# Waits of GpSimd behind VectorE, and sums that read PSUM, in a two-layer attention trunk on one core

## The chip, the core and the metric

The kernel runs on one core of a Trainium2 chip. A core has engines with queues of their own that run side by side: TensorE (PE in the rows; PEld is its weight load), VectorE (DVE), ScalarE (ACT), GpSimd (POOL) and SyncE (SP), which issues the DMA transfers here. SBUF is the working memory of all of them, PSUM the memory into which TensorE writes; this kernel uses it as eight banks of 128 x 512 fp32. The metric is the device time of one execution in microseconds (us); three executions of the kernel before took 1012.47, 1005.16 and 1011.17 us, median 1011.17.

## The reference

The input is x, 256 x 1024 in fp32. There are two layers, and each adds three things to x: a SwiGLU feed-forward of 1024 to 2816 to 1024, a mixer, and a second feed-forward, every one between two RMS norms. Layer 1's mixer is plain attention over 16 heads with a bias by distance. Layer 0's mixer, the even one, is where the change lies. One projection h @ w_in (1024 to 3368 columns) gives:

- A: four differential heads. Each has two query and two key vectors of 64 and one value of 128. With p1 and p2 the two masked softmaxes, the weights are p1 - lam * p2.
- B: eight heads of 64 that look at the best 64 keys alone, as an indexer chooses them (8 small heads of 32, relu, a weighted sum, top 64).
- Queries and keys of A, B and the indexer are turned by rotary embedding first.

```
def apply_rope(x, cos, sin):
    x1, x2 = jnp.split(xf, 2, axis=-1)
    return jnp.concatenate([x1 * c - x2 * s, x2 * c + x1 * s], axis=-1)

s = jnp.einsum('bqhcd,bkhcd->bhcqk', qblk, kf) * scale
p = masked_softmax(s, mask)
w = p[:, :, 0] - lam * p[:, :, 1]
```

## The kernel before, in words

Every matrix product is made of three fp32r products: a high and a low part of each operand, high x high, high x low and low x high. So each weight tile passes ScalarE, which casts it to a high part wh (L277), and then VectorE, which makes the low part wl = raw - wh (L279). In the even mixer wl may be made by VectorE or by GpSimd, 512 columns at a time. The 256 tokens are two tiles t of 128.

Nothing is written down in the order in which it runs. The program calls op(engines, us, fn, w, r, pos, port) for each piece of work, which records it with an estimated duration and a due place pos. Plan.issue then plays the whole list through on estimated durations: an engine that is free takes, of the pieces that are ready and whose buffers are free, the one due first, and its instruction is issued. An instruction thus stands in its engine's queue where that play put it, and on the chip each queue runs in that fixed order and waits at semaphores for its inputs. The buffers are counted: `ps` has 4 PSUM banks and `y` 4.

One rule of the planner concerns the change. VectorE and GpSimd are taken to share a port to SBUF. A piece marked port=True is not begun in the play while another marked piece runs on either engine:

```
if o["port"] and e != "ACT" and port > now + 1e-9:
    fits = False
    event(port, "", None)
```

This orders the estimated times alone. On the chip no wait stands between the two engines for it.

Marked pieces are the wl subtractions (L279), products and sums of two SBUF tensors in the norms (L471, L529, L544, L550, L555), the scaling of softmax weights in B (L841), the sum at the end of rope (L744) and the sum of a differential head (L983).

rope (L729 on) takes a projection's PSUM bank b. L736 writes b * cos to an SBUF tile a, two L740 write the sine parts to an SBUF tile r, and L744 adds r to a; the planner chooses VectorE or GpSimd for the sum. TensorE transposes the sum (L427) into another bank, and ScalarE and VectorE split that into high and low parts (L363/L365, L369/L371). Ten ropes are computed: two of 288 columns for the indexer (after which GpSimd copies 96 columns, L894) and eight of 512.

A differential head h takes its scores (L795) in two banks of `ps`. soft() adds the mask and takes the negated maximum (L812, VectorE, from PSUM to an SBUF tile e), then the exponentials with their sums (L816, ScalarE, in place in e). The pieces L977 to L979 work on columns of 128 x 2 in SBUF and carry no mark; L983 adds the second softmax times a factor to the first, in SBUF. Then come the transposes of the sum (L427), their split (L369, pt) and the product with the values (L417 to L419, y<-blk,pt).

Within the even mixer VectorE also makes the indexer's scores (L923) and takes the top 64 in eight rounds of L930 and L931 for each t; these have one SBUF tensor as input, or PSUM and SBUF.

Of the kernel before, what the change touches and what calls it, by code (L numbers as in the profile page):

```python
# [14 lines left out]
P = 128  # L15
# [37 lines left out]
class Plan:  # L53
# [36 lines left out]
        self.pos += us  # L90
        return self.last

    def issue(self):
        free = dict(SLOTS)
        eng = {e: 0.6 for e in LAT}
        heap = {e: [] for e in LAT}
        ev, n, port = [], 0, 0.0
        todo = len(self.ops)

        def push(o):  # L100
            for e in o["eng"]:
                heapq.heappush(heap[e], (o["pos"], o["id"], o))

        def event(t, kind, x):
            nonlocal n
            n += 1
            heapq.heappush(ev, (t, n, kind, x))

        for o in self.ops:
            if o["n"] == 0:  # L110
                push(o)
        event(0.6, "", None)
        now = 0.0
        while ev:
            now = ev[0][0]
            while ev and ev[0][0] <= now + 1e-9:
                _, _, kind, x = heapq.heappop(ev)
                if kind == "ready":
                    push(x)
                elif kind == "free":  # L120
                    free[x.tag] += x.n
            for e in heap:
                if eng[e] > now + 1e-9:
                    continue
                skip, got, late = [], None, None
                while heap[e]:
                    z = heapq.heappop(heap[e])
                    o = z[2]
                    if o["end"] is not None:
                        continue  # L130
                    need = [q for q in o["refs"] if q.t is None]
                    fits = all(free[q.tag] >= sum(p.n for p in need if p.tag == q.tag) for q in need)
# [4 lines that stand above are left out]
                    for q in o["refs"]:  # L137

                        if q.tag in BANKS and q.used[0] != e and q.used[1] > now + 1e-9:
                            fits = False  # L140
                            event(q.used[1], "", None)
                    if fits and o["safe"] <= now + 1e-9:
                        got = o
                        break
                    if fits and late is None:
                        late = z
                    skip.append(z)
                if got is None and late is not None:
                    got = late[2]
                    skip.remove(late)  # L150
                for z in skip:
                    heapq.heappush(heap[e], z)
                if got is None:
                    continue
                o = got
                need = [q for q in o["refs"] if q.t is None]
                for q in need:
                    free[q.tag] -= q.n
                    q.t = q.make()
                us = o["us"] if len(o["eng"]) == 1 else o["us"][e]  # L160
                o["fn"]() if len(o["eng"]) == 1 else o["fn"](e)
                if o["port"] and e != "ACT":
                    port = now + us
                end = eng[e] = o["end"] = now + us
                todo -= 1
                event(end, "", None)
                for q in o["refs"]:
                    q.used = (e, end + 0.1)
                for d in o["out"]:
                    d["n"] -= 1  # L170
                    at = end + (OWN[e] if d["eng"] == (e,) else o["lat"])
                    d["ready"] = max(d["ready"], at)
                    if d["eng"] == ("PE",) != (e,):
                        d["safe"] = max(d["safe"], at + SAFE)
                    if d["n"] == 0:
                        d["ready"] = max(d["ready"], now)
                        event(d["ready"], "ready", d)
                for q in o["refs"]:
                    q.left -= 1
                    if q.left == 0:  # L180
                        event(end + 0.05, "free", q)
        assert todo == 0, [(o["eng"], o["pos"], o["n"], [q.tag for q in o["refs"]])
                           for o in self.ops if o["end"] is None][:20]
        return now
# [6 lines left out]
def n_dve(n, fast=False):  # L191
    return 0.07 + n * (0.00052 if fast else 0.00104)
# [3 lines left out]
def trunk_kernel(  # L196
# [531 lines left out]

    def rope(b, tab, t, n, half, fa, fk):  # L729

        g = n // (2 * half)
        a, r = t2(), t2()
        v4 = lambda q: q.t[:, :n].rearrange("p (g two h) -> p g two h", two=2, h=half)
        def c1():
            c = tab.t[:, t, 0, :].rearrange("p (two h) -> p two h", two=2).unsqueeze(1).to_broadcast([P, g, 2, half])
            nc.vector.scalar_tensor_tensor(v4(a), v4(b), fa(), c, op0=ALU.mult, op1=ALU.mult)  # L736
        op(DVE, n_dve(n) + 0.06, c1, r=[b, tab] + fk, w=[a])
        def c2(i):
            s = tab.t[:, t, 1, i * half:(i + 1) * half].unsqueeze(1).to_broadcast([P, g, half])
            nc.vector.scalar_tensor_tensor(v4(r)[:, :, i, :], v4(b)[:, :, 1 - i, :], fa(), s, op0=ALU.mult, op1=ALU.mult)  # L740
        for i in range(2):
            op(DVE, n_dve(n // 2) + 0.06, lambda i=i: c2(i), r=[b, tab] + fk, w=[(r, i)])
        def add(e):
            (nc.vector if e == "DVE" else nc.gpsimd).tensor_add(a.t[:, :n], a.t[:, :n], r.t[:, :n])  # L744
        op(DVE + POOL, {"DVE": n_dve(n), "POOL": 0.11 + n * 0.00233}, add, r=[(r, 0), (r, 1)], w=[a], port=True)
        return a

    class HL:

# [53 lines left out]

        op(ACT, 1.4, lambda: nc.scalar.activation(warm.t, nhalf.t[:, 0:1], fn), r=[nhalf], w=[warm], after=after)

    def soft(bs, hh, madd, mk, r, c, pos):

        e = t2()
        mx = sm(2)
        for t in range(2):  # L810
            def mxf(t=t):
                nc.vector.tensor_tensor_reduce(e.t[:, QS[t]], bs[hh].t[:, QS[t]], madd(t), -1.0, 1e38, ALU.add, ALU.min,  # L812
                                               mx.t[:, t:t + 1])
            op(DVE, n_dve(KL[t]), mxf, r=[(bs[hh], t)] + mk, w=[(e, t), (mx, t)], pos=pos)
            def ex(t=t):
                nc.scalar.activation(e.t[:, QS[t]], e.t[:, QS[t]], AF.Exp, bias=mx.t[:, t:t + 1], scale=-1.0,  # L816
                                     accum_out=r.t[:, c + t:c + t + 1])
# [61 lines left out]
    def even(xT, nxt):  # L879
# [90 lines left out]
        for h in range(4):  # L970
            pos = pA + h * PERA
            r, ri = sm(4), sm(4)
            bs = scores(aq.v, aq.k(0) + aq.k(1), h, h, pos, trs[h - 2:h - 1] if h > 1 else ())
            es = [soft(bs, c, cm, [cmask], r, 2 * c, pos) for c in range(2)]
            def comb(h=h, ri=ri, r=r):

                nc.vector.reciprocal(ri.t[:, 2:4], r.t[:, 2:4])  # L977
# [3 lines left out]
            for t in range(2):  # L981
                def ad(t=t, e=es, ri=ri):
                    nc.vector.scalar_tensor_tensor(e[0].t[:, QS[t]], e[1].t[:, QS[t]], ri.t[:, 2 + t:3 + t],  # L983
                                                   e[0].t[:, QS[t]], op0=ALU.mult, op1=ALU.add)
                op(DVE, n_dve(KL[t]) + 0.06, ad, r=[ri, (es[1], t)], w=[(es[0], t)], pos=pos, port=True)
            z = new_pt(1)
            trs.append(transp_p(es[0], z, 0, pos))
            def pv(h=h, z=z):
# [131 lines left out]
    for l in range(2):  # L1120
        for p in range(3):
# [11 lines left out]
            else:  # L1133
                ffn(l, p // 2, xT, nxt)
            xT = z
    pl.issue()


# [48 lines left out]
```

## Time and profile before

| what | before |
|---|---|
| three executions | 1012.47, 1005.16, 1011.17 us; median 1011.17 us |
| the profiled execution | 1006.86 us |
| its span, first to last instruction | 1005.1 us |
| TensorE busy | 991.6 us, 99% of the span |
| VectorE, ScalarE, GpSimd busy | 725.7, 607.4 and 85.2 us |
| DMA moved | 185.52 MB, 185 GB/s |
| mean granted clock of TensorE | 0.999 |

All times of rows are those of the profiled execution, counted from the span's start. A matmul row's length runs past the start of the next matmul, since matmuls are pipelined: where 512-column matmuls follow each other they start 0.23 us apart while each row has 0.39 us. A row with "xN" merges N instructions of the same kind that follow each other. What stands in brackets is how long the engine was idle before the row, and what ended that. The even mixer runs from about 195 to 322 us of the span.

### The profile page before, as it was taken

How to read it: one execution, taken by the hardware profiler on the slowest of the kernel's cores; microseconds unless marked ns; L12 is line 12 of the kernel's file. 1: busy time of each engine (PE TensorE's matmuls, PEld its weight loads, DVE VectorE, ACT ScalarE, POOL GpSimd, SP SyncE). 2: the span in 40 equal slices, each digit the busy share in tenths (PEclk: the TensorE clock that was granted, in tenths of full speed). 3: DMA queues.
4: the chain of work that ended last, by engine and by line, in shares of the span. 5: the costliest groups of instructions: out<-in, count | busy, mean ns of one | idle time of the engine just before them, and what ended most of it. 6: DMA issues, size and time to landing. Idle time of an engine off the chain costs nothing.

```text
span 1005.1 us, 15484 instructions
## 1 busy us (share of the span) xinstructions
PE 991.6 (99%) x5435; PEld 847.6 (84%) x5435; DVE 725.7 (72%) x1537; ACT 607.4 (60%) x1376; POOL 85.2 (8%) x107
## 2 busy tenths in 40 slices
PE   9999999999999999999999999999999999999997
PEld 8888888877888988888888888888888888888886
DVE  7766668689888676677577667676778877666682
ACT  8555556556588555565466555576578856555661
POOL 1000000156531100000020000001100010000000
PEclk9999999999999999999999999999999999999999
DMA  9866665555545567666467666664775447666621
GB/s 343 293 184 178 196 191 144 161 178 167 167 138 157 166 218 200 192 187 190 146 209 247 180 182 192 195 178 149 224 267 159 124 148 251 188 179 194 192 87 42
DMA packets 125933, 185.52 MB, mean 185 GB/s; under 512 B 6040, under 2 KB 93984, under 8 KB 125856
## 3 DMA queue, kind: packets, MB, share of 16 engines
q1 hardware_dynamic: 125856, 184.54, 59.9%
q8 instruction: 42, 0.69, 0.3%
q14 instruction: 35, 0.29, 0.1%
HBM read 183.47 MB, written 1.05 MB: 184 GB/s over the span
## 4 chain that ended last, share of the span: by engine, by line
PE 89%; DVE 7%; ACT 2%; issue 1%; DMA 1%; POOLq 0%; DVEq 0%; ACTq 0%; POOL 0%
PE ps L387 26%; PE ps L389 14%; PE y L417 9%; PE y L418 9%; PE y L419 9%; PE ps L412 4%; PE ps L409 4%; PE ps L410 4%; PE ps L427 2%; DVE wl L279 2%; PE ps L417 2%; PE ps L418 2%; PE ps L419 2%; PE ps L795 1%; DMA g<-in_norm_g_dram 1%
## 5 line engine op out<-in xcount | busy, mean ns | idle before, releaser
L279 DVE TENSOR_TENSOR wl<-raw,wh 128x512 fp32r<-128x512 f32 (+2 forms) x636 | 418.0, 689 | 133.5 <-ACT wh L277 91.3
L277 ACT CAST wh<-raw 128x512 fp32r<-128x512 f32 (+2 forms) x668 | 378.8, 615 | 124.5 <-issue 70.1
L387 PE MATMUL ps<-xT,wh 128*128 128x512 f32 x1152 | 290.4, 393 | 0.0
L387 PEld LDWEIGHTS ps<-xT,wh 128*128 128x128 f32 x1152 | 208.1, 189 | 38.0
L389 PEld LDWEIGHTS ps<-xT,wl 128*128 128x128 f32 x1152 | 157.5, 190 | 11.6
L389 PE MATMUL ps<-xT,wl 128*128 128x256 f32 x1152 | 162.8, 283 | 0.0
L417 PE MATMUL y<-wh,blk 128*128 128x512 f32 x352 | 138.1, 392 | 0.0
L418 PE MATMUL y<-wl,blk 128*128 128x512 f32 x352 | 137.4, 390 | 0.0
L419 PE MATMUL y<-wh,blk 128*128 128x512 f32 x352 | 137.1, 390 | 0.0
L409 PE MATMUL ps<-wh,xT 128*128 128x512 f32 (+2 forms) x320 | 107.6, 351 | 0.1
L410 PE MATMUL ps<-wl,xT 128*128 128x512 f32 (+2 forms) x320 | 106.1, 347 | 0.8 <-DVE wl L279 0.3
L396 DVE TENSOR_TENSOR t<-ps,t 128x256 f32<-128x256 f32 x144 | 60.6, 421 | 44.3 <-ACT t L395 42.8
L395 ACT COPY t<-ps 128x256 f32<-128x256 f32 x144 | 53.6, 373 | 51.8 <-PE ps L389 48.0
L453 POOL TENSOR_TENSOR sm<-sm 128x1 f32<-128x1 f32 x24 | 14.9, 621 | 777.9 <-ACT t L534 721.4
L419 PEld LDWEIGHTS y<-wh,blk 128*128 128x128 f32 x352 | 66.1, 188 | 13.9
L417 PEld LDWEIGHTS y<-wh,blk 128*128 128x128 f32 x352 | 66.2, 188 | 12.8
L418 PEld LDWEIGHTS y<-wl,blk 128*128 128x128 f32 x352 | 66.2, 188 | 12.6
L410 PEld LDWEIGHTS ps<-wl,xT 128*128 128x128 f32 x320 | 60.6, 189 | 8.8 <-DVE wl L279 2.3
L412 PE MATMUL ps<-wh,xT 128*128 128x512 f32 (+2 forms) x320 | 67.6, 347 | 0.0
L409 PEld LDWEIGHTS ps<-wh,xT 128*128 128x128 f32 x320 | 60.5, 189 | 8.0 <-ACT xT L363 0.5
L680 ACT ACTIVATE t<-t 128x256 f32<-128x256 f32 x64 | 26.8, 418 | 55.2 <-DVE t L679 55.2
L412 PEld LDWEIGHTS ps<-wh,xT 128*128 128x128 f32 x320 | 51.3, 189 | 6.6
(148 smaller groups left out, 1030.7 us busy)
## 6 DMA issues: line engine op xcount, KB each, us to landing
raw<-in_wd_dram SPq DMA_DIRECT2D x88, 512.0 KB, 4.2
raw<-in_wg_dram SPq DMA_DIRECT2D x86, 512.0 KB, 4.4
raw<-in_wu_dram SPq DMA_DIRECT2D x86, 512.0 KB, 4.5
raw<-in_ew_in_dram SPq DMA_DIRECT2D x24, 512.0 KB, 4.6
raw<-in_ow_in_dram SPq DMA_DIRECT2D x24, 512.0 KB, 4.5
g<-in_norm_g_dram SPq DMA_DIRECT2D x11, 512.0 KB, 5.7
raw<-in_ew_out_dram SPq DMA_DIRECT2D x8, 512.0 KB, 3.7
raw<-in_ow_out_dram SPq DMA_DIRECT2D x8, 512.0 KB, 4.0
```

The lines of the kernel that those rows point to most:

```text
L277: nc.scalar.copy(ref.t[0][:, sl], raw.t[:, sl])
L279: (nc.vector if e == "DVE" else nc.gpsimd).tensor_sub(ref.t[1][:, sl], raw.t[:, sl], ref.t[0][:, sl].bitcast(F32))
L387: nc.tensor.matmul(b.t, w()[0], xT.both[:, k].rearrange("p j c -> p (j c)"), start=k == 0, stop=False)
L389: nc.tensor.matmul(b.t[:, 0:S], w()[1], xT.t[0][:, k, :], start=False, stop=k == KT - 1)
L395: op(ACT, n_act(S, True), lambda: nc.scalar.copy(dst.t[:, sl], b.t[:, S:512]), r=[b], w=[(dst, sl.start)])
L396: op(DVE, n_dve(S), lambda: nc.vector.tensor_add(dst.t[:, sl], b.t[:, 0:S], dst.t[:, sl]), r=[b], w=[(dst, sl.start)])
L409: nc.tensor.matmul(o(), ah, bh, start=k == 0, stop=False)
L410: nc.tensor.matmul(o(), ah, bl, start=False, stop=False)
L412: nc.tensor.matmul(o(), al, bh, start=False, stop=k == KT - 1)
L417: nc.tensor.matmul(o, ah, bh, start=start, stop=False)
L418: nc.tensor.matmul(o, ah, bl, start=False, stop=False)
L419: nc.tensor.matmul(o, al, bh, start=False, stop=stop)
```

## The change

It has four parts.

1. The planner remembers the last marked instruction that it issued on VectorE (held). Whenever it issues a marked instruction on GpSimd, it adds a dependence on that one, so that GpSimd waits at a semaphore until it has ended. Nothing is added to VectorE's instructions.
2. rope keeps its cosine part in the projection's own bank: the two sine parts are made first, then b is multiplied by cos in place, and the sum r = b + r reads PSUM and SBUF. It is for VectorE alone and has no mark. One SBUF tile less is used; the bank is released after the sum.
3. The second softmax of a differential head stays in its scores' bank: L812 and L816 write where they read. The bank is released after L983.
4. L983 thus reads PSUM and SBUF and loses its mark.

```
-    def issue(self):
+    def issue(self, tc):
...
-        ev, n, port = [], 0, 0.0
+        ev, n, port, held = [], 0, 0.0, None
...
                 if o["port"] and e != "ACT":
                     port = now + us
+                    done = tc.nc.cur_bb.bb.instructions[-1]
+                    if e == "DVE":
+                        held = done
+                    elif held is not None:
+                        tc.add_manual_dep(done, held.name, mybir.DependencyInfo(mybir.DependencyClass.Sync, mybir.DependencyReason.DATA),
+                                          reason="port")
...
     def rope(b, tab, t, n, half, fa, fk):
-        a, r = t2(), t2()
+        r = t2()
...
-            nc.vector.scalar_tensor_tensor(v4(a), v4(b), fa(), c, op0=ALU.mult, op1=ALU.mult)
-        op(DVE, n_dve(n) + 0.06, c1, r=[b, tab] + fk, w=[a])
...
         for i in range(2):
             op(DVE, n_dve(n // 2) + 0.06, lambda i=i: c2(i), r=[b, tab] + fk, w=[(r, i)])
-        def add(e):
-            (nc.vector if e == "DVE" else nc.gpsimd).tensor_add(a.t[:, :n], a.t[:, :n], r.t[:, :n])
-        op(DVE + POOL, {"DVE": n_dve(n), "POOL": 0.11 + n * 0.00233}, add, r=[(r, 0), (r, 1)], w=[a], port=True)
-        return a
...
+            nc.vector.scalar_tensor_tensor(v4(b), v4(b), fa(), c, op0=ALU.mult, op1=ALU.mult)
+        op(DVE, n_dve(n) + 0.06, c1, r=[tab] + fk, w=[b])
+        op(DVE, n_dve(n), lambda: nc.vector.tensor_add(r.t[:, :n], b.t[:, :n], r.t[:, :n]), r=[b], w=[(r, 0), (r, 1), r])
+        return r
...
-    def soft(bs, hh, madd, mk, r, c, pos):
-        e = t2()
+    def soft(bs, hh, madd, mk, r, c, pos, inplace=False):
+        e = bs[hh] if inplace else t2()
...
-            es = [soft(bs, c, cm, [cmask], r, 2 * c, pos) for c in range(2)]
+            es = [soft(bs, c, cm, [cmask], r, 2 * c, pos, c == 1) for c in range(2)]
...
-                op(DVE, n_dve(KL[t]) + 0.06, ad, r=[ri, (es[1], t)], w=[(es[0], t)], pos=pos, port=True)
+                op(DVE, n_dve(KL[t]) + 0.06, ad, r=[ri, (es[1], t)], w=[(es[0], t)], pos=pos)
```

Because the planner's inputs differ, the order differs on four engines, from the start of the even mixer's ropes to its end; SyncE's order is the same. In the changed program lines above the insertion at L164 are shifted: L277 is L284, L279 is L286, L369 and L371 are L376 and L378, L427 is L434; rope's sine parts are L744, its cosine L749, its sum L751; L977 to L979 are L983 to L985, and L983 is L989.

The first place is VectorE's queue between the rope of the indexer's second tile (ps_2186) and that of the first head group's second tile (ps_2235, in the changed program ps_2234). wl, raw and wh are the parts of the weight tiles, blk the split queries. Before:

```order
L740 SCALAR_TENSOR_TENSOR t_371_2245<-ps_2186,sm_2118,r_82 128x9x16 x2
L279 TENSOR_TENSOR wl_2232<-raw_2057,wh_2231 128x512
L279 TENSOR_TENSOR wl_2225<-raw_2036,wh_2224 128x512
L279 TENSOR_TENSOR wl_2232<-raw_2057,wh_2231 128x512
L279 TENSOR_TENSOR wl_2252<-raw_2084,wh_2251 128x512
L279 TENSOR_TENSOR wl_2263<-raw_2129,wh_2262 128x512
L371 SCALAR_TENSOR_TENSOR blk_2268<-ps_2254,blk_2267 128x4x128
L736 SCALAR_TENSOR_TENSOR t_386_2306<-ps_2235,sm_2118,r_81 128x512
L740 SCALAR_TENSOR_TENSOR t_388_2314<-ps_2235,sm_2118,r_81 128x8x32 x2
L744 TENSOR_TENSOR t_386_2306<-t_386_2306,t_388_2314 128x512
```

The changed program there:

```order
L751 TENSOR_TENSOR t_368_2239<-ps_2186,t_368_2239 128x288
L286 TENSOR_TENSOR wl_2222<-raw_2036,wh_2221 128x512
L286 TENSOR_TENSOR wl_2230<-raw_2057,wh_2229 128x512
L286 TENSOR_TENSOR wl_2250<-raw_2084,wh_2249 128x512
L286 TENSOR_TENSOR wl_2261<-raw_2129,wh_2260 128x512
L378 SCALAR_TENSOR_TENSOR blk_2266<-ps_2252,blk_2265 128x4x128
L376 TENSOR_TENSOR blk_2208<-ps_2282,blk_2207 128x3x128
L286 TENSOR_TENSOR wl_2261<-raw_2129,wh_2260 128x512
L744 SCALAR_TENSOR_TENSOR t_385_2317<-ps_2234,sm_2118,r_81 128x8x32 x2
L749 SCALAR_TENSOR_TENSOR ps_2234<-ps_2234,sm_2118,r_81 128x512
L751 TENSOR_TENSOR t_385_2317<-ps_2234,t_385_2317 128x512
```

The indexer's sum, which GpSimd made before, now stands on VectorE ahead of the subtractions, the split of the indexer's second tile has come forward into this stretch, and one of the five subtractions has moved behind it.

The second place is GpSimd's queue over the same stretch. Before:

```order
L744 TENSOR_TENSOR t_354_2157<-t_354_2157,t_356_2173 128x288
L894 COPY t_354_2157<-t_354_2157 128x96
L744 TENSOR_TENSOR t_360_2196<-t_360_2196,t_361_2202 128x512
L279 TENSOR_TENSOR wl_2225<-raw_2036,wh_2224 128x512
L279 TENSOR_TENSOR wl_2252<-raw_2084,wh_2251 128x512
L279 TENSOR_TENSOR wl_2263<-raw_2129,wh_2262 128x512
L744 TENSOR_TENSOR t_370_2240<-t_370_2240,t_371_2245 128x288
L894 COPY t_370_2240<-t_370_2240 128x96
```

The changed program:

```order
L900 COPY t_354_2157<-t_354_2157 128x96
L286 TENSOR_TENSOR wl_2222<-raw_2036,wh_2221 128x512
L286 TENSOR_TENSOR wl_2230<-raw_2057,wh_2229 128x512
L900 COPY t_368_2239<-t_368_2239 128x96
L286 TENSOR_TENSOR wl_2250<-raw_2084,wh_2249 128x512
L286 TENSOR_TENSOR wl_2294<-raw_2169,wh_2293 128x512
```

The sums are gone. By the semaphores of the changed program, wl_2222 there waits for L536 (blk_2189, the product ahead of the second rope), wl_2250 for VectorE's first wl_2261, and wl_2294 for its second.

The third place is VectorE's queue at the sums of differential heads 1 and 2. Before, they stand behind the last round of the second top 64 and its mask (L933), next to each other:

```order
L740 SCALAR_TENSOR_TENSOR t_474_2811<-ps_2693,sm_1963,r_81 128x8x32 x2
L933 TENSOR_SCALAR selm<-t_405_2415 128x256
L983 SCALAR_TENSOR_TENSOR t_441_2640<-t_444_2648,sm_2677,t_441_2640 128x128
L983 SCALAR_TENSOR_TENSOR t_441_2640<-t_444_2648,sm_2677,t_441_2640 128x256
L983 SCALAR_TENSOR_TENSOR t_462_2737<-t_466_2753,sm_2779,t_462_2737 128x128
L983 SCALAR_TENSOR_TENSOR t_462_2737<-t_466_2753,sm_2779,t_462_2737 128x256
L744 TENSOR_TENSOR t_473_2798<-t_473_2798,t_474_2811 128x512
```

In the changed program head 1's sum follows its factors:

```order
L983 RECIPROCAL sm_2688<-sm_2644 128x2
L984 SCALAR_TENSOR_TENSOR sm_2688<-sm_2688,nlam,sm_2644 128x2
L985 TENSOR_TENSOR rsq<-sm_2644 128x2
L378 SCALAR_TENSOR_TENSOR blk_2587<-ps_2582,sm_2118,blk_2586 128x512
L989 SCALAR_TENSOR_TENSOR t_435_2636<-ps_2616,sm_2688,t_435_2636 128x128
L989 SCALAR_TENSOR_TENSOR t_435_2636<-ps_2616,sm_2688,t_435_2636 128x256
L936 MAX m_1_91<-t_400_2413 128x8
```

Head 1's sum has moved ahead of most rounds of the second top 64 (L936 and L937 there), and reads the bank ps_2616.

## Rows read from the trace of the kernel before

**Rows 1.** The page's first part: busy time, share of the span and number of instructions of each engine.

```profile
PE 991.6 (99%) x5435; PEld 847.6 (84%) x5435; DVE 725.7 (72%) x1537; ACT 607.4 (60%) x1376; POOL 85.2 (8%) x107
```

**Rows 2.** The waits of TensorE in the whole span: what waited, for whom, us in total, times, the longest.

```profile
PE ps L427 <- DVE t L744: 2.5, 2, 1.7
...
PE ps L427 <- DVE pt L369: 0.7, 1, 0.7
PE ps L427 <- POOL t L744: 0.5, 1, 0.5
PE ps L795 <- DVE blk L371: 0.3, 1, 0.3
```

**Rows 3.** The timeline of TensorE at these waits: start us, length us, line, operation, shape, count, and in brackets the idle time before and its releaser.

```profile
209.69 0.39 PE L409 MATMUL ps<-wh,xT 128*128 128x512 f32 x1
209.93 0.40 PE L410 MATMUL ps<-wl,xT 128*128 128x512 f32 x1
210.84 0.66 PE L427 MATMUL ps<-ident,t 128*128 128x128 f32 x4 [0.52 <-POOL t L744]
...
221.67 0.63 PE L427 MATMUL ps<-ident,t 128*128 128x128 f32 x4 [1.67 <-DVE t L744]
...
230.35 0.63 PE L427 MATMUL ps<-ident,t 128*128 128x128 f32 x4 [0.87 <-DVE t L744]
...
249.36 0.32 PE L795 MATMUL ps<-KBh,blk 64*128 64x128 f32 x1 [0.32 <-DVE blk L371]
...
263.02 0.55 PE L427 MATMUL ps<-ident,t 128*128 128x128 f32 x3 [0.72 <-DVE pt L369]
```

**Rows 4.** The timeline of VectorE, same columns.

```profile
206.90 0.69 DVE L529 TENSOR_TENSOR blk<-X,g 128x512 f32<-128x512 f32 x1 [2.32 <-DMA g<-in_norm_g_dram]
207.51 0.75 DVE L736 SCALAR_TENSOR_TENSOR t<-ps,sm,r 128x512 f32<-128x512 f32 x1
208.17 0.87 DVE L740 SCALAR_TENSOR_TENSOR t<-ps,sm,r 128x256 f32<-128x256 f32 x2
208.96 0.68 DVE L529 TENSOR_TENSOR blk<-X,g 128x512 f32<-128x512 f32 x1
209.55 0.55 DVE L369 TENSOR_TENSOR blk<-ps,blk 128x384 fp32r<-128x384 f32 x1
...
211.13 6.67 DVE L279 TENSOR_TENSOR wl<-raw,wh 128x512 fp32r<-128x512 f32 x5
217.72 0.68 DVE L371 SCALAR_TENSOR_TENSOR blk<-ps,blk 128x512 fp32r<-128x512 f32 x1
218.32 0.73 DVE L736 SCALAR_TENSOR_TENSOR t<-ps,sm,r 128x512 f32<-128x512 f32 x1
...
219.88 1.65 DVE L744 TENSOR_TENSOR t<-t,t 128x512 f32<-128x512 f32 x1
221.45 3.56 DVE L279 TENSOR_TENSOR wl<-raw,wh 128x512 fp32r<-128x512 f32 x4
...
229.52 0.69 DVE L744 TENSOR_TENSOR t<-t,t 128x512 f32<-128x512 f32 x1
...
246.21 1.19 DVE L978 SCALAR_TENSOR_TENSOR sm<-sm,nlam,sm 128x2 f32<-128x2 f32 x1
...
253.58 1.33 DVE L979 TENSOR_TENSOR rsq<-sm 128x2 f32<-128x2 f32 x1
...
259.29 1.40 DVE L983 SCALAR_TENSOR_TENSOR t<-t,sm,t 128x128 f32<-128x128 f32 x4
...
261.21 1.29 DVE L279 TENSOR_TENSOR wl<-raw,wh 128x512 fp32r<-128x512 f32 x2
```

**Rows 5.** The timeline of GpSimd, same columns.

```profile
209.19 1.60 POOL L744 TENSOR_TENSOR t<-t,t 128x512 f32<-128x512 f32 x1 [3.69 <-DVE t L740]
210.75 1.29 POOL L279 TENSOR_TENSOR wl<-raw,wh 128x512 fp32r<-128x512 f32 x1
212.72 3.32 POOL L279 TENSOR_TENSOR wl<-raw,wh 128x512 fp32r<-128x512 f32 x2 [0.68 <-ACT wh L277]
216.00 1.24 POOL L744 TENSOR_TENSOR t<-t,t 128x288 f32<-128x288 f32 x1
...
246.09 10.04 POOL L279 TENSOR_TENSOR wl<-raw,wh 128x512 fp32r<-128x512 f32 x8 [3.61 <-ACT wh L277]
```

**Rows 6.** VectorE's instructions between 200 and 340 us, grouped by line and shape: count, busy us in all, mean ns of one, idle us before.

```profile
L279 DVE TENSOR_TENSOR wl<-raw,wh 128x512 fp32r<-128x512 f32 x41 | 32.1, 824 | 2.7 <-ACT wh L277 2.6
...
L539 DVE TENSOR_TENSOR t<-y,g 128x512 f32<-128x512 f32 x4 | 2.7, 684 | 0.0
...
L923 DVE SCALAR_TENSOR_TENSOR t<-y,wI,t 128x256 f32<-128x256 f32 x7 | 3.3, 473 | 0.0
...
L983 DVE SCALAR_TENSOR_TENSOR t<-t,sm,t 128x256 f32<-128x256 f32 x4 | 1.9, 480 | 0.0
...
L529 DVE TENSOR_TENSOR blk<-X,g 128x512 f32<-128x512 f32 x2 | 1.4, 688 | 2.3 <-DMA g<-in_norm_g_dram 2.3
```

**Rows 7.** ScalarE's squares of 512 columns between 200 and 340 us, from PSUM (y) and from SBUF (X), same columns.

```profile
L475 ACT ACTIVATE t<-X 128x512 f32<-128x512 f32 x5 | 3.1, 631 | 1.7 <-DVE X L555 1.7
...
L534 ACT ACTIVATE t<-y 128x512 f32<-128x512 f32 x4 | 2.4, 596 | 1.5 <-PE y L419 1.5
```

More of the change, by code (lines that the diff above doesn't have):

```diff
@@ L731, in rope @@
         g = n // (2 * half)
-        a, r = t2(), t2()
+        r = t2()
         v4 = lambda q: q.t[:, :n].rearrange("p (g two h) -> p g two h", two=2, h=half)
-        def c1():
-            c = tab.t[:, t, 0, :].rearrange("p (two h) -> p two h", two=2).unsqueeze(1).to_broadcast([P, g, 2, half])
-            nc.vector.scalar_tensor_tensor(v4(a), v4(b), fa(), c, op0=ALU.mult, op1=ALU.mult)
-        op(DVE, n_dve(n) + 0.06, c1, r=[b, tab] + fk, w=[a])
         def c2(i):
@@ L742, in rope, with c1 @@
             op(DVE, n_dve(n // 2) + 0.06, lambda i=i: c2(i), r=[b, tab] + fk, w=[(r, i)])
-        def add(e):
-            (nc.vector if e == "DVE" else nc.gpsimd).tensor_add(a.t[:, :n], a.t[:, :n], r.t[:, :n])
-        op(DVE + POOL, {"DVE": n_dve(n), "POOL": 0.11 + n * 0.00233}, add, r=[(r, 0), (r, 1)], w=[a], port=True)
-        return a
+        def c1():
+            c = tab.t[:, t, 0, :].rearrange("p (two h) -> p two h", two=2).unsqueeze(1).to_broadcast([P, g, 2, half])
+            nc.vector.scalar_tensor_tensor(v4(b), v4(b), fa(), c, op0=ALU.mult, op1=ALU.mult)
+        op(DVE, n_dve(n) + 0.06, c1, r=[tab] + fk, w=[b])
+        op(DVE, n_dve(n), lambda: nc.vector.tensor_add(r.t[:, :n], b.t[:, :n], r.t[:, :n]), r=[b], w=[(r, 0), (r, 1), r])
+        return r
     class HL:
@@ L813, in mxf @@
                                                mx.t[:, t:t + 1])
-            op(DVE, n_dve(KL[t]), mxf, r=[(bs[hh], t)] + mk, w=[(e, t), (mx, t)], pos=pos)
+            op(DVE, n_dve(KL[t]), mxf, r=([] if inplace else [(bs[hh], t)]) + mk, w=[(e, t), (mx, t)], pos=pos)
             def ex(t=t):
@@ L1135, in trunk_kernel @@
             xT = z
-    pl.issue()
+    pl.issue(tc)
 def kernel(**inputs):
```

## The prediction

> **What bounds the kernel.** I read the page's first part first: TensorE is busy for 991.6 of the 1005.1 us, every other engine for much less [rows 1]. So time can come from two places alone: work taken off TensorE, and moments in which TensorE waits. The change removes no matmul; its TensorE instructions are the same in another order. So I went to TensorE's waits. In the even mixer there are four kinds: for a rope sum on VectorE, 2.5 us in two waits; for a rope sum on GpSimd, 0.5; for the split of a softmax transpose (pt), 0.7; for a bank that VectorE still read (blk, L371), 0.3 [rows 2]. That is 4.0 us, 0.4% of the span, and the ceiling of what this change can give unless the new order shortens something that TensorE's view does not show.
>
> Then I asked why VectorE is late there. The reader is to compare lengths of the same instruction. Two L279 take 1.29 us, start to start 0.60 each, while GpSimd rests; five of them take 6.67 us from 211.13, where 0.09 + 5 x 0.60 = 3.1 would do, and four take 3.56 instead of 2.5 [rows 4]. L744 takes 0.69 us at 229.52 and 1.65 at 219.88. L978 and L979, which handle two columns, take 1.19 and 1.33 us at 246.21 and 253.58 [rows 4]. In each of those moments GpSimd works on two SBUF tensors [rows 5] (the first 246.09 to 256.13). Through 41 L279 the mean is 824 ns [rows 6]. In the same moments instructions that read PSUM keep their length: L736 has 0.73 us at 218.32 beside GpSimd, 0.75 at 207.51 without [rows 4]. So a VectorE instruction with two SBUF tensors loses up to one GpSimd instruction's time; one with a PSUM operand loses nothing.
>
> **The change, part by part.** The sums go against the profiled execution, 1006.86 us, of which 1005.1 are the span and 1.8 lie around it.
>
> *First rope sum, wait 0.52.* Before, GpSimd's sum takes 1.60 us from 209.19, ends at 210.79, and TensorE goes on at 210.84 [rows 3, 5]. Now VectorE makes it. From L529 at 206.90, which waits for a DMA in both programs, the starts in rows 4 give 0.61 (L529) + 0.79 (two sine parts) + 0.59 (L529) + 0.66 (cosine) + 0.5 (L369) + 0.69 (sum) = 3.84, so 210.7. Gain 0.1; I count nothing.
>
> *Second rope sum, wait 1.67.* TensorE is ready at 221.67 - 1.67 = 220.0 [rows 3]. VectorE's new order from 210.7: the pieces of the 288-column rope, which take 211.13 - 209.55 - 0.5 = 1.1 us in rows 4, and its sum, an estimate of 0.4 (0.69 x 288/512): 212.2. Then five L279 at 0.60, L371 0.60, the indexer's split 0.5, sine parts 0.79, cosine 0.66, sum 0.69: 6.2 us, so 218.4 if nothing collides. That is 1.6 us ahead of TensorE. What collides: GpSimd's first two subtractions now fall beside the rope, which needs no port; its third waits for VectorE's fourth L279 and can meet only the fifth. I take one collision, half a GpSimd subtraction of 1.29 us [rows 5], 0.65: 219.0, and the wait of 1.67 is gone. Bounds: if all of the old loss stayed (6.67 - 3.1 = 3.6), 222.0, 0.3 us worse than before.
>
> *Third rope sum, wait 0.87.* TensorE was ready at 230.35 - 0.87 = 229.5. It now comes 1.67 earlier, and by the new order eight 512-column matmuls fewer stand ahead of these transposes, 0.24 x 8 = 1.9 at most [rows 3]: 225.9. VectorE from 219.0: three L279 1.8, one collision 0.65, L371 0.6, sine 0.79, cosine 0.66, one L923 about 0.4, sum 0.69: 224.6. The wait goes too; with old collisions in full (3.56 - 2.5 = 1.1 instead of 0.65) it still goes.
>
> *Ten sums on VectorE instead of five.* Five come over from GpSimd: three of 512 and two of 288, 3 x 0.69 + 2 x 0.4 = 2.9 us on an engine whose rows from 206.90 to 211.13 and from 217.72 to 221.45 follow each other with hardly a gap [rows 4]. Ahead of the three waits they are counted above; behind them stands one of the five, in front of a transpose that TensorE reaches late anyway; nothing more is added.
>
> *Second softmax in PSUM.* No row has VectorE writing PSUM. Nearest: L923 reads PSUM for 256 columns at 473 ns, L983 reads SBUF alone at 480 [rows 6]; so zero, with bounds of zero and eight L812 and eight L983 at 0.1 us, a generous 1.6 us, of which only what stands before a wait counts. ScalarE's exponentials in place in PSUM: a square from PSUM takes 596 ns, from SBUF 631 [rows 7]; zero, ScalarE is not late here. What moves is the sums' place: heads 1 and 2 had theirs together at 259.29, four L983 in 1.40 us [rows 4], behind the top 64, and the pt wait at 263.02 follows from that rush [rows 3]. Now each follows its factors. In exchange, a scores' bank is held until L983, and TensorE's scores of heads 1 and 2 need the bank of a value projection that VectorE empties (L371) late. I let these cancel: the 1.0 us of pt and bank waits stays in other places. Bounds: all of it gone (gain 1.0), or the stops of rival B.
>
> *GpSimd's waits.* Queued behind each are further subtractions, each of 1.29 us; TensorE needs their wl several us later, since weights are made some 9 us ahead by the planner's due times. One instruction is tight: the 96-column copy behind two subtractions, wanted by TensorE after ten matmuls from 211.2, so at 213.6. The two start at about 209.1, after L529, and end by 211.7; the copy waits for the sum at 212.2. Nothing is added. If that cover is gone the price is one subtraction, 1.3 us.
>
> Sum: -1.67 - 0.87 = -2.5 us; 1006.86 becomes 1004.3. The profiled execution lies 4.3 us below the median of the three runs. The four executions known are 1005.16, 1006.86, 1011.17 and 1012.47; their middle is 1009.0. From there the forecast is **1006.5 us**. Everything behind the mixer is bound by TensorE and should shift by the same amount.
>
> [...] L539 reads PSUM and SBUF at 684 ns, L529 two SBUF tensors at 688 [rows 6]. [...]
>
> **Rivals.**
>
> A. *The waits do not part the engines.* Only GpSimd waits; a VectorE subtraction that comes while GpSimd works is late as before, and L978 and L979 have no mark. For: rows 4 show VectorE, not GpSimd, losing. Against: in the queues GpSimd now stands behind VectorE's groups. If collisions stay whole, the second sum comes 0.3 later and only the third wait goes: -0.87 + 0.3 = -0.6, 1008.4. This is also the case in which the change does not do what it says. [...]
>
> B. *Banks become the bound* (slower). There are four ps banks. Scores of heads 1, 2 and 3 may each stop until VectorE has emptied a bank. Per head that is L371, 0.68, and two L983, half of 1.40 [rows 4], about 1.4 us, and the old stop at 249.36 was of this kind, 0.32 [rows 3]. It decides when VectorE reaches L983 of a head after TensorE has come to the scores of the next but one. Three full stops cost 4.2, against the gain of 2.5: +1.7, 1010.7. For: VectorE has no slack there. Against: before, the sums of heads 1 and 2 could come together as late as 259.29 [rows 4] without stopping any scores, and the planner now gives them an earlier place.
>
> C. *All four kinds of wait go*: -4.0, 1005.0.
>
> **Numbers.** Chances: the forecast 0.48, A 0.22, B 0.18, C 0.12. The three runs before span 7.3 us with nothing changed, more than any of these cases, so the range is that of the runs moved by the cases: the lowest run with C, 1005.16 - 4.0 = 1001, up to the highest run, 1012.5, which leaves out the upper part of B. About 1% (10 us) is what a measurement of this kernel can tell from no change; no case reaches it by itself, neither way, since the waits in reach are 4.0 us. Faster by over 1% takes C or more and low runs: 0.05. Slower takes B beyond its price and high runs: 0.03. Within 1%: 0.92.
>
> **What would show it.** In the changed profile: TensorE's waits for L751 should be down to the first, about 0.5 us; five L286 from about 212 should take near 3.7 us instead of 6.67; no L751 should be longer than 0.75 us, beside GpSimd or not; L983 to L985 (small columns) may still be long. A: L286 on VectorE still averages above 800 ns in the mixer. B: waits of L801 for L378 or L989 of over 1 us each. The prediction is wrong if TensorE waits longer than 4 us in the mixer, or if a wl from GpSimd is what a matmul waits for.

## The result and the profile after

The changed kernel takes 1002.31 us (median of 6 runs, 1001.88 to 1002.68). The kernel before, timed again beside it, has a median of 1010.52 us over 6 runs (1005.16 to 1012.47). The ratio is 0.9929, with a 95% interval from 0.9906 to 0.9952: 0.7% faster, a gain of 8.2 us between the medians. Between the two profiled executions, 1006.86 and 1002.35 us, it is 4.5 us. The changed kernel's runs lie within 0.8 us of each other, where those of before span 7.3.

The first part of the page after, busy time of each engine, answers to [rows 1]:

```profile
PE 990.5 (99%) x5435; PEld 847.6 (85%) x5435; DVE 723.2 (72%) x1542; ACT 607.8 (61%) x1376; POOL 76.8 (8%) x102
```

TensorE's waits in the whole span after (what waited, for whom, us in total, times, the longest) answer to [rows 2]:

```profile
PE ps L347 <- DVE selm L345: 1.1, 1, 1.1
PE ps L434 <- DVE blk L557: 0.8, 2, 0.4
PE ps L416 <- ACT wh L284: 0.6, 2, 0.4
PE ps L417 <- DVE wl L286: 0.3, 1, 0.3
```

All four kinds of wait of [rows 2] are gone, for rope sums on either engine, for pt and for the bank. What is left stands at the start of the kernel and behind the mixer. VectorE's timeline after (start us, length us, line, operation, count) answers to [rows 4]:

```profile
206.05 0.69 DVE L536 TENSOR_TENSOR blk<-X,g 128x512 f32<-128x512 f32 x1 [0.63 <-DMA g<-in_norm_g_dram]
...
209.17 0.68 DVE L751 TENSOR_TENSOR t<-ps,t 128x512 f32<-128x512 f32 x1
...
211.50 2.79 DVE L286 TENSOR_TENSOR wl<-raw,wh 128x512 fp32r<-128x512 f32 x4
...
215.28 1.09 DVE L286 TENSOR_TENSOR wl<-raw,wh 128x512 fp32r<-128x512 f32 x1
...
217.99 0.69 DVE L751 TENSOR_TENSOR t<-ps,t 128x512 f32<-128x512 f32 x1
218.60 2.22 DVE L286 TENSOR_TENSOR wl<-raw,wh 128x512 fp32r<-128x512 f32 x3
...
223.49 0.68 DVE L751 TENSOR_TENSOR t<-ps,t 128x512 f32<-128x512 f32 x1
...
260.54 1.27 DVE L985 TENSOR_TENSOR rsq<-sm 128x2 f32<-128x2 f32 x1
```

Five subtractions take 2.79 + 1.09 = 3.88 us instead of 6.67, and no rope sum is longer than 0.69. TensorE's transposes of the same three 512-column ropes start without any wait, 0.7 to 1.1 us behind the ends of their sums (209.85, 218.68, 224.17); they answer to [rows 3]:

```profile
210.62 0.60 PE L434 MATMUL ps<-ident,t 128*128 128x128 f32 x4
...
219.39 0.60 PE L434 MATMUL ps<-ident,t 128*128 128x128 f32 x4
...
225.22 0.60 PE L434 MATMUL ps<-ident,t 128*128 128x128 f32 x4
```

GpSimd's subtractions now come behind groups of VectorE's: the row at 214.52 behind 211.50 + 2.79 = 214.29, the row at 216.51 behind 215.28 + 1.09 = 216.37. What stands in brackets names pieces of ScalarE as the last to end, so VectorE is not alone in setting these starts. GpSimd's subtractions still meet a later one of VectorE, as the 1.09 shows:

```profile
209.32 2.55 POOL L286 TENSOR_TENSOR wl<-raw,wh 128x512 fp32r<-128x512 f32 x2 [3.50 <-DVE blk L376]
...
214.52 1.30 POOL L286 TENSOR_TENSOR wl<-raw,wh 128x512 fp32r<-128x512 f32 x1 [1.98 <-ACT blk L370]
216.51 2.56 POOL L286 TENSOR_TENSOR wl<-raw,wh 128x512 fp32r<-128x512 f32 x2 [0.68 <-ACT wh L284]
```

**A ruler for the mixer.** GpSimd's small rstd sums stand just ahead of the mixer and just behind its last big projection, in every kernel here. Their starts before and after, as rows of GpSimd's timeline:

```profile
201.05 0.64 POOL L453 TENSOR_TENSOR sm<-sm 128x1 f32<-128x1 f32 x1 [3.26 <-DVE sm L448]
...
323.02 0.20 POOL L453 TENSOR_TENSOR sm<-sm 128x1 f32<-128x1 f32 x1 [19.57 <-ACT t L534]
```

```profile
201.52 0.64 POOL L460 TENSOR_TENSOR sm<-sm 128x1 f32<-128x1 f32 x1 [3.26 <-DVE sm L455]
...
318.34 0.20 POOL L460 TENSOR_TENSOR sm<-sm 128x1 f32<-128x1 f32 x1 [22.52 <-ACT t L541]
```

The stretch takes 121.97 us before and 116.82 after: 5.15 less. Of that 4.10 are the five waits of [rows 3]; the other 1.05 would be 0.2 for each wait, which is an estimate: what makes it up is not shown. The rest of the span is the same, 883.1 and 883.6 us. So the profiles account for 4.5 us of run time, and the question for the experiments is double: which part of the change did it, and where the other 3.7 us of the 8.2 come from.

### The profile page after: what moved, and what is told of

It is laid out like the page before. It is cut to its first block, busy times and chain, and to the rows that moved or that the text cites. A ratio compares the mean times of both kernels' runs of the same rounds, so it can differ in the third digit from the quotient of the medians.

```text
span 1000.4 us, 15479 instructions
## 1 busy us (share of the span) xinstructions
PE 990.5 (99%) x5435; PEld 847.6 (85%) x5435; DVE 723.2 (72%) x1542; ACT 607.8 (61%) x1376; POOL 76.8 (8%) x102
## 3 DMA queue, kind: packets, MB, share of 16 engines
HBM read 183.47 MB, written 1.05 MB: 184 GB/s over the span
## 4 chain that ended last, share of the span: by engine, by line
PE 95%; DVE 2%; ACT 1%; DMA 1%; issue 0%; SPq 0%; POOLq 0%; DVEq 0%; POOL 0%; ACTq 0%
PE ps L394 26%; PE ps L396 14%; PE y L424 9%; PE y L425 9%; PE y L426 9%; PE ps L416 6%; PE ps L419 6%; PE ps L417 6%; PE ps L434 3%; PE ps L425 2%; PE ps L424 2%; PE ps L426 2%; PE ps L801 1%; DVE wl L286 1%; DMA raw<-in_wg_dram 1%
## 5 line engine op out<-in xcount | busy, mean ns | idle before, releaser
L286 DVE TENSOR_TENSOR wl<-raw,wh 128x512 fp32r<-128x512 f32 (+2 forms) x636 | 414.8, 683 | 133.4 <-ACT wh L284 92.2
L284 ACT CAST wh<-raw 128x512 fp32r<-128x512 f32 (+2 forms) x668 | 377.9, 614 | 115.6 <-issue 66.6
```

Of the source, the lines that this page charges most:

```text
L284: nc.scalar.copy(ref.t[0][:, sl], raw.t[:, sl])
L286: (nc.vector if e == "DVE" else nc.gpsimd).tensor_sub(ref.t[1][:, sl], raw.t[:, sl], ref.t[0][:, sl].bitcast(F32))
```

## Experiments

All medians below stand against runs of the kernel before on the same chip; the ruler is the mixer's stretch in the profiled execution. In each pair of experiments that differs by GpSimd's waits alone, TensorE, VectorE, ScalarE and GpSimd have the same order of instructions.

**The unchanged kernel again, twice.** No edit.

> The kernel before, unchanged, profiled once more: its runs lie between 1005 and 1012.5, the changed kernel's within 0.8. Theory 1 (the time hangs on how VectorE and GpSimd happen to meet): another execution has TensorE's waits at the same rope sums, but of other lengths, and the span differs from 1005.1 by the difference of these waits (with about 0.25 us more lost beside each). Theory 2 (the scatter is of something else, such as transfers): the waits in the mixer are 4.0 us again, and a longer span shows longer stretches elsewhere.

> As before_again1: a third look at the unchanged kernel, to see whether waits for rope sums of 2.5 to 9 us go with spans of 1004 to 1010.

They came at 1013.44 and 1011.15 us, ruler 126.38 and 125.24. The first also entered the mixer 2.2 us later: at the start of the kernel TensorE waited twice for the high part of a weight, 1.0 us in all, and its granted clock was 0.91 over the first 20 us, where the first profile has 1.00. The ruler leaves that out. Against [rows 2] the waits for pt and the bank are the same; of the rope waits the first (0.52) is gone, the second is 0.68 and 0.30 in place of 1.67, and the third has grown. TensorE's timeline of the first of them at the second and third 512-column rope:

```profile
222.41 0.63 PE L427 MATMUL ps<-ident,t 128*128 128x128 f32 x4 [0.68 <-DVE t L744]
...
234.20 1.09 PE L427 MATMUL ps<-ident,t 128*128 128x128 f32 x4 [3.95 <-DVE t L744]
...
240.35 0.40 PE L409 MATMUL ps<-wh,xT 128*128 128x512 f32 x1
```

The third wait is 3.95 us instead of 0.87 (in the other profile 3.95 as well), and the four transposes behind it take 1.09 instead of 0.63. The windows of the same stretch (start and end, length, busy us and count of PE, PEld, DVE, ACT and POOL, granted clock, DMA share, GB/s) tell why:

```profile
226.00:230.00 4.00, 4.00 (x18) 3.17 (x18) 3.96 (x9) 1.29 (x5) 0.00 (x0) 1.00 0.65 194
230.00:234.20 4.20, 0.25 (x2) 0.03 (x1) 4.06 (x6) 1.54 (x3) 3.62 (x3) 0.91 0.64 212
234.20:236.00 1.80, 1.80 (x7) 1.61 (x8) 1.49 (x6) 0.67 (x2) 0.98 (x1) 0.50 0.63 239
236.00:238.00 2.00, 2.00 (x23) 1.35 (x25) 1.59 (x5) 0.95 (x2) 0.00 (x0) 0.50 0.77 222
238.00:240.00 2.00, 2.00 (x16) 1.49 (x13) 1.89 (x7) 1.34 (x3) 0.76 (x1) 0.50 0.14 48
240.00:241.00 1.00, 1.00 (x5) 0.84 (x4) 1.00 (x6) 1.00 (x3) 1.00 (x2) 0.85 0.00 0
```

TensorE idles, and its granted clock falls to 0.50 for some 7 us, 6 of them behind the wait. From the transposes to the fifth 512-column matmul of the next projection it takes 240.35 - 234.20 = 6.15 us; in the first profile of before the same matmuls go from 230.35 [rows 3] to

```profile
233.78 0.39 PE L409 MATMUL ps<-wh,xT 128*128 128x512 f32 x1
```

which is 3.43. So the clock costs 2.72 us; the other profile has 5.93, so 2.50. The third wait grows through meetings that tenths of a microsecond decide. VectorE and GpSimd in that execution:

```profile
221.57 0.69 DVE L744 TENSOR_TENSOR t<-t,t 128x512 f32<-128x512 f32 x1
222.18 4.67 DVE L279 TENSOR_TENSOR wl<-raw,wh 128x512 fp32r<-128x512 f32 x4
...
230.77 1.62 DVE L279 TENSOR_TENSOR wl<-raw,wh 128x512 fp32r<-128x512 f32 x1
232.31 1.74 DVE L744 TENSOR_TENSOR t<-t,t 128x512 f32<-128x512 f32 x1
```

```profile
221.69 3.42 POOL L279 TENSOR_TENSOR wl<-raw,wh 128x512 fp32r<-128x512 f32 x2 [0.80 <-ACT wh L277]
230.57 4.61 POOL L279 TENSOR_TENSOR wl<-raw,wh 128x512 fp32r<-128x512 f32 x3 [5.47 <-ACT wh L277]
```

Here GpSimd begins its three subtractions 0.2 us before VectorE's last one, which then takes 1.62 us, and the rope sum behind it 1.74. In the first profile VectorE had started both ahead of GpSimd's next three, and the sum took 0.69 [rows 4] and the subtraction 0.68:

```profile
228.92 0.68 DVE L279 TENSOR_TENSOR wl<-raw,wh 128x512 fp32r<-128x512 f32 x1
```

```profile
219.71 2.94 POOL L279 TENSOR_TENSOR wl<-raw,wh 128x512 fp32r<-128x512 f32 x2 [0.54 <-ACT wh L277]
229.81 4.04 POOL L279 TENSOR_TENSOR wl<-raw,wh 128x512 fp32r<-128x512 f32 x3 [7.15 <-ACT wh L277]
```

There the four L279 ahead of them had taken 3.56 [rows 4] and not 4.67. The three differences, 1.11, 0.94 and 1.05, are the 3.1 us by which the wait grew. The first of them goes with the second rope: here its sum begins 0.12 us before GpSimd's pair of subtractions, takes 0.69, and leaves the pair to the four L279; in the first profile it began 0.17 us behind the pair and took 1.65 itself. Neither theory had this right: the place was the rope sums, as theory 1 has it, but the waits alone are 1.5 us longer than in the first profile, and the ruler 4.4; the clock is most of the rest. By the mean clock it is also what most runs look like. Of 69 runs of before timed beside these experiments, 8 have a mean granted clock of 0.999 over the span, like the first profile, and their median is 1006.7 us; 50 have 0.997 or less. The 11 at 0.998 have a median of 1009.2, so the clock is not all of it. The changed kernel's six runs all have 0.998 or 0.999.

**The waits alone.** The kernel before with the hunks of `issue` and nothing else:

```
                     port = now + us
+                    done = tc.nc.cur_bb.bb.instructions[-1]
+                    if e == "DVE":
+                        held = done
+                    elif held is not None:
+                        tc.add_manual_dep(done, held.name, ...)
```

> The kernel before with GpSimd's waits alone; rope and softmax as they were. Theory 1 (VectorE instructions are lengthened by GpSimd's two-SBUF-tensor work, and that makes TensorE wait): the L279 of VectorE in the mixer come down from a mean of 824 ns to 700 to 740, the second and third rope waits (1.67 and 0.87) go, but the sums that GpSimd still makes are held back by its waits, so about 1 us of waits for them stays or comes new: median 1003 to 1007. Theory 2 (the planner's new order took the time, the lengthening fell where VectorE had slack): order and waits as before, median 1008 to 1012, TensorE's waits in the mixer 3.5 to 4.5 us.

1003.47 us, ratio 0.9935 [0.9913, 0.9957], a gain of 6.4 us; ruler 118.48, runs within 2.1 us. VectorE's subtractions between 200 and 340 us have a mean of 724 ns. The five of [rows 4] and the two waits that are left in the mixer:

```profile
210.19 4.16 DVE L286 TENSOR_TENSOR wl<-raw,wh 128x512 fp32r<-128x512 f32 x5
```

```profile
245.88 0.32 PE L802 MATMUL ps<-KBh,blk 64*128 64x128 f32 x1 [0.27 <-DVE blk L378]
259.52 0.55 PE L434 MATMUL ps<-ident,t 128*128 128x128 f32 x3 [0.71 <-DVE pt L376]
```

All rope waits are gone, though the sums are still where they were, and the pt and bank waits stay near their old sizes (0.72 and 0.32). Theory 1 holds, save that GpSimd's held-back sums made no wait. Most of the change's gain is here.

**No waits, PSUM alone.** The changed kernel without the lines above.

> The changed kernel without GpSimd's waits: same order, rope and second softmax in PSUM. Theory 1: the subtractions of the two engines meet again, L286 on VectorE at a mean of 800 ns or more in the mixer, and TensorE waits again for 1 to 2 us where a late split or rope part stands behind five of them: median 1003.5 to 1006. Theory 2: as the changed kernel, 1002.3 within 0.5, with no wait of TensorE in the mixer.

1005.80 us, ratio 0.9967 [0.9953, 0.9981]; ruler 120.75. The subtractions of VectorE between 200 and 340 us (count, busy us, mean ns, idle before), here and in the changed kernel:

```profile
L279 DVE TENSOR_TENSOR wl<-raw,wh 128x512 fp32r<-128x512 f32 x41 | 33.6, 856 | 2.2 <-ACT wh L277 2.2
```

```profile
L286 DVE TENSOR_TENSOR wl<-raw,wh 128x512 fp32r<-128x512 f32 x45 | 31.2, 732 | 5.9 <-ACT wh L284 5.9
```

The order of the instructions is that of the changed kernel; what differs is who meets whom. TensorE waits 1.50 for a rope sum at 220.69, 1.28 for a head's sum at 265.15 and 0.39 for a key block: theory 1, and the order alone is not what did it. Against before this is still a gain of 4.1 us, so what the parts give alone, 6.4 and 4.1, overlaps in the 8.2 of the whole.

**Rope in PSUM alone**, waits and softmax as before. Of its edit, the sum:

```
...
-        op(DVE + POOL, {...}, add, r=[(r, 0), (r, 1)], w=[a], port=True)
+        op(DVE, n_dve(n), lambda: nc.vector.tensor_add(r.t[:, :n], b.t[:, :n], r.t[:, :n]), r=[b], w=[...])
```

> The kernel before with rope's cosine part in PSUM and its sum on VectorE; second softmax and waits as before. Theory 1: the rope sums no longer take 1.65 us beside GpSimd, but the subtractions ahead of them do meet GpSimd: of 3.0 us of rope waits half goes, the waits for pt and the bank (1.0) stay: 1005 to 1008. Theory 2: the order of the rope is what mattered, the 3.0 go: 1002.5 to 1004.

1005.27 us, ratio 0.9958 [0.9944, 0.9972]; ruler 120.14, runs within 2.2 us. Three rope waits are left, 0.36, 0.94 and 1.55, and none for pt or a bank. Both theories erred in detail. The time fits the first: the long wait, and with it the low clock, is gone (the mean over the span is 0.999), and the sums, which now have a PSUM operand, were not held up (eight of 512 columns at a mean of 685 ns). The order differs from before's as well, and this run does not part the two.

**The second softmax in PSUM alone.**

```
-            es = [soft(bs, c, cm, [cmask], r, 2 * c, pos) for c in range(2)]
+            es = [soft(bs, c, cm, [cmask], r, 2 * c, pos, c == 1) for c in range(2)]
```

> The kernel before with the second softmax of a head in PSUM alone; rope and waits as before. Both theories: the rope waits (3.0 us) stay; the wait for pt, 0.7, and perhaps that for the bank, 0.3, go: median 1 us under that of before, 1008 to 1011. A rival (banks become the bound): waits of the scores for a bank of over 1 us in all, 1011 or more.

1008.61 us (1005.81 to 1013.34), ratio 0.9989 [0.9972, 1.0006]: no difference that can be told; ruler 122.74. Its profile has the single wait

```profile
230.97 0.63 PE L427 MATMUL ps<-ident,t 128*128 128x128 f32 x4 [3.96 <-DVE t L744]
```

and behind it the clock at 0.50, though later and for less long than in the two profiles of before: it has 0.74 from 231 to 233 us, 0.50 from 233 to 235 and 0.81 from 235 to 236, some 3 us of 0.50 in all. The waits for pt and the bank are gone, and no scores wait for a bank: the part does what it should, hidden under the rope's scatter.

**Waits and rope, softmax as before.**

> The changed kernel with the second softmax back in SBUF: waits of GpSimd and rope in PSUM. Theory 1 (the softmax part takes away the pt and bank waits alone, 1.0 us): 1003.0 to 1003.8, against 1002.3 with it and 1003.5 with the waits alone, so rope in PSUM adds 0.3 or less once GpSimd waits. Theory 2 (rope in PSUM takes them, by the order that it brings): 1002.3, and the softmax part is worth nothing.

1003.18 us, ratio 0.9938 [0.9916, 0.9960]; ruler 118.40, against 118.48 with the waits alone and 116.82 with all. So once GpSimd waits, rope in PSUM adds nothing that shows, and the softmax part is worth 1.6 us of the ruler. Its only mixer wait is 1.55 for a rope sum at 255.88, in place of pt's and the bank's. Theory 1 has the time, not the kind of wait.

**One wait alone.** The kernel before, where the condition of the waits is narrowed to one instruction, the first of the three subtractions that began at 230.57 above; it waits for the third rope sum. The edit is shown against the waits alone:

```
-                    elif held is not None:
+                    else:
+                        self.npool = getattr(self, "npool", 0) + 1
+                    if e == "POOL" and self.npool == 10 and held is not None:
```

> The kernel before with one wait alone: the first of GpSimd's three subtractions behind VectorE's third 512-column rope sum waits for that sum. Theory 1 (the scatter and the upper two thirds of the time of before come from the third rope sum, which meets these subtractions in most executions: wait 3.95 and then a TensorE clock of 0.50): the 4 us wait goes, at most 2 are left, the clock stays at 1.00 behind it, and the median is 1005 to 1007.5 with 2.5 us of scatter. Theory 2 (the meetings add up over the mixer and no one place decides): less than a quarter of the 6.4 us that all the waits gave, 1008 to 1010.

1006.96 us (1004.78 to 1008.35), ratio 0.9968 [0.9954, 0.9981]; ruler 119.90. A single wait gives 3.3 us, half of the 6.4 that all of them give. The third rope wait is 1.94 in its profile, and the clock stays at 1.00: theory 1. That profile is of its fastest run, and two of its twelve runs have a mean clock of 0.996.

**TensorE's wait priced.** The changed kernel, with sine parts of the third rope made seven or thirteen times more, so that its sum comes late:

```
+            for _ in range(8 if i == 1 and n == 512 and len(ropes) == 3 else 1):
                 nc.vector.scalar_tensor_tensor(v4(r)[:, :, i, :], ...)
```

> The changed kernel with seven more of the third rope's sine parts, 0.39 us each, ahead of its sum: TensorE's slack there is 1.05 us (sum ends at 224.17, transpose at 225.22), so it should wait for 7 x 0.39 - 1.05 = 1.7 us. Theory 1 (a wait of this length costs itself and no clock): 1002.3 + 1.7 to 2.2 = 1004 to 1004.5, granted clock 1.00 behind the wait. Theory 2 (any wait brings the clock down to half for some us): 1006 to 1007.

> As stall_2 with thirteen more sine parts: a wait of 13 x 0.39 - 1.05 = 4.0 us, as long as that of the two slower profiles of before. Theory 1: the clock falls to 0.50 behind it for about 6 us, so the wait costs 4.0 + 0.3 + 2.7: 1002.3 + 7 = 1009 to 1010. Theory 2 (the clock fell there for another reason): 1006 to 1007, clock 1.00.

The parts took 0.51 us from start to start, not 0.39, so the waits came at 2.50 and 5.59. With 5.59 the median is 1010.39 us, and the ruler 8.1 us longer than in the changed kernel. The windows of that profile:

```profile
226.00:228.00 2.00, 0.00 (x0) 0.00 (x0) 1.86 (x5) 0.00 (x0) 0.00 (x0) 1.00 0.73 254
228.00:230.00 2.00, 0.00 (x0) 0.00 (x0) 1.93 (x5) 0.00 (x0) 0.00 (x0) 0.67 0.05 20
230.00:232.00 2.00, 1.52 (x6) 1.42 (x7) 1.74 (x5) 0.36 (x1) 0.00 (x0) 0.50 0.00 0
232.00:234.00 2.00, 2.00 (x7) 1.52 (x6) 1.84 (x5) 0.22 (x1) 0.00 (x0) 0.50 0.00 0
234.00:236.00 2.00, 2.00 (x7) 1.46 (x5) 0.66 (x4) 1.52 (x3) 1.06 (x1) 0.62 0.00 0
236.00:238.00 2.00, 2.00 (x29) 1.57 (x29) 1.66 (x5) 2.00 (x5) 2.00 (x3) 1.00 0.05 12
```

The wait is made by hand here, with GpSimd idle beside it, and the clock falls all the same: theory 1. With the 2.50 wait the profile shows a clock of 1.00 throughout and a ruler 3.7 us longer (2.50, and 0.68 at the first rope). Its nine runs part in two: four with a mean clock of 0.999 take 1004.6 to 1005.7 us, five with 0.996 or 0.997 take 1006.1 to 1008.1. The median, 1006.09, falls into theory 2's range, but the wait came longer than both theories had it. By the mean clock, then, it came down in the five and not in the four; one execution alone was profiled.

**No GpSimd subtractions.** The changed kernel, L286 on VectorE alone.

> The changed kernel with every L286 on VectorE: GpSimd takes none, so nothing is lengthened, but VectorE gets some 35 subtractions more of 0.6 us in the mixer, 21 us on an engine with about 8 us idle between 200 and 300. Theory 1 (GpSimd's help is needed, only not beside VectorE): TensorE waits for splits or sums by 5 us or more, 1007 to 1015. Theory 2 (the help is worth no more than the meeting costs, and the planner shifts the subtractions to later idle time): 1002 to 1004.

1008.17 us, ratio 0.9986 [0.9974, 0.9998]; ruler 123.25. A subtraction takes 679 ns here, the length without meetings, and yet 5.9 us are lost against the changed kernel (6.4 of the ruler): VectorE is busy for 20.00 of the 20 us from 210 to 230, and TensorE waits 1.26 us at 306.49 behind a late normalization. Theory 1 has the time, though TensorE's waits in the mixer are 2.6 us and not 5; behind the one at 306.49 the clock is at 0.50 as well, for some 3 us.

**Waits in both directions.** VectorE's port instructions wait for GpSimd's last one too.

> The changed kernel, and VectorE's port instructions wait for GpSimd's last one as well. Theory 1 (the meetings that are left are where VectorE has slack; TensorE's waits in the mixer are already 0): no gain, 1002.3 within 0.7, L286 on VectorE at 690 to 735 ns. Rival (each wait costs VectorE the rest of a subtraction of 1.29 us and delays the work in PSUM behind it): TensorE waits for a rope or a split by 1 to 3 us, 1003.5 to 1006.

1002.93 us over 4 runs, ratio 0.9937 [0.9912, 0.9962]; ruler 116.78 against 116.82. The subtractions come down to 686 ns and nothing is gained: the meetings that the change leaves fall where VectorE has slack. No version tried beats the changed kernel by anything that can be told.

## Why the prediction was right, and where it was wrong

The forecast was 1006.5 us in a range from 1001 to 1012.5, within 1% of before. The measured 1002.3 lies in it, and the direction and the class were right. The size was not: a gain of 2.5 us was forecast, and the profiles show 4.5, the medians 8.2. Two things hid this. The range was 11.5 us wide, since it carried the scatter of before, and the measured time lies 1.3 us above its lower end. And the base of 1009.0 was 1.5 us under the median of 1010.5, so that of the 5.7 us missing in the gain only 4.2 show in the time.

**What bounds it.** TensorE's waits in the mixer, and behind them VectorE's two-SBUF-tensor instructions held up by GpSimd: right, shown by the waits alone (subtractions at 724 ns against 824, rope waits gone, order unchanged) and by their absence (856 ns, waits back).

**The ceiling of 4.0 us** was the step that failed. It was read from one execution, and that was one of the mildest. In both other profiles the third rope wait is 3.95 us, with 2.7 and 2.5 us of half clock behind it. By the ruler the one profile of the changed kernel is 5.2, 9.6 and 8.4 us shorter than the three executions, and as far as three profiles tell, that is where the medians' other 3.7 us come from. The sentence that the runs span 7.3 us "with nothing changed, more than any of these cases" took the effect for noise: that scatter was the thing that the change removes.

**First rope sum.** "I count nothing"; the wait of 0.52 went. The working was right, 3.80 us from L536 to the sum's end where 3.84 was worked out, but g's transfer landed 0.85 us earlier than in the first profile, 206.05 against 206.90. In the waits alone, where GpSimd still makes this sum, the wait is gone too, and neither other profile of before has it. So it was a matter of one execution's transfer.

**Second and third.** Sums at 219.0 and 224.6 were worked out; they end at 218.68 and 224.17. TensorE reaches the third transpose at 225.22, worked out 225.9. Five subtractions "near 3.7" took 3.88. This was the part with the most terms, and its outcome held, partly by luck: from the first sum's end to the second's 8.3 was worked out and 8.83 measured (209.85 to 218.68), and the early transfer made up for it.

**Ten sums on VectorE.** Behind the three waits stood two of the five sums that came over, where the prediction counts one: GpSimd made them at 234.92 and 266.09 in the first profile. No wait came of either.

**pt and bank.** "I let these cancel" was wrong: 1.0 us of waits did not move to other places, it went. With the softmax back in SBUF 1.6 us of the ruler come back. No score waits for a bank, so rival B (0.18) fell. Its condition, VectorE reaching a head's sum late, did not arise, since the sums now follow their factors.

**Second softmax in PSUM at zero:** right for VectorE. L751 with a PSUM operand has a mean of 683 ns, L744 took 0.69 us undisturbed [rows 4]; L989 takes 471 ns for 256 columns where L983 took 480 [rows 6]. Neither is longer with the PSUM operand.

**GpSimd's waits at zero:** right. No matmul of the mixer waits for a wl of GpSimd.

**Rivals.** A (0.22) fell with 732 ns against its 800. C (0.12), all four kinds of wait gone, is what happened, and its 1005.0 was still 2.7 too high: its gain of 4.0 was half of the 8.2 measured, and only its low base kept it that near.

## To carry to other kernels

When the runs of a kernel scatter by many times what its siblings do, profile it more than once before pricing a change: the scatter may be the effect, and one profile shows one of its ends. Here VectorE and GpSimd met some tenths of a microsecond earlier or later, and one wait of TensorE was 0.87 us in one execution and 3.95 in two others; holding the order by waits alone gave 6.4 us, moving the work without them 4.1. A wait of TensorE is priced with what its clock does afterwards, 2.7 and 2.5 us behind the two waits of 3.95; the mean granted clock of each run gives a hint of that without a profile, but not of the place, as the slow start in one of the repeated profiles shows.

## What was not expected of the hardware

- In the profiles, waits of TensorE of 1.67 us (before), 1.55 (waits and rope), 1.94 (one wait) and 2.50 (seven more sine parts) left the clock at 1.00. Waits of 3.95 us (twice) and 5.59 went with 0.50 for some 7 us, which cost 2.7 and 2.5 us in the first two; one of 3.96 us was followed by some 3 us of it. A wait of 1.26 us was followed by some 3 us of it too, with TensorE busy for 0.67 of the 2 us from 305 to 307 (no GpSimd subtractions). So the length of the wait alone did not decide.
- An instruction of two columns was held up like one of 512: L985 takes 1.27 us at 260.54 beside GpSimd, whose subtractions begin at 260.50, and 0.15 to 0.16 the other three times.
- ScalarE's exponential of 256 columns in place takes 448 ns in PSUM, 498 in SBUF. The prediction had read 596 against 631 for squares and counted nothing for it.
- Two VectorE instructions that read what the one ahead of them wrote started later: L751 stands 0.79 us behind the start of L749 (217.20 to 217.99), where another row behind L749 starts after 0.67 (208.04 to 208.71). It is not of PSUM alone: before, the sum L744 at 219.88 starts 0.50 behind the sine part that it reads from SBUF, and the two sine parts stand 0.40 apart.
